# A hybrid decoder trunk in float32: one MLP weight block in four gets its remainder from an accumulating DMA instead of VectorE

## The chip, the cores and the metric

The kernel runs on one core of one Trainium2 chip. The metric is device microseconds of one execution. The profile is of one execution, recorded by the hardware; its times are microseconds from the first instruction unless ns is said. Engines: PE is TensorE (PEld its weight loads), DVE is VectorE, ACT is ScalarE, POOL is GpSimd, SP is SyncE, which here issues only DMAs.

## What is computed

Two decoder layers on 256 tokens of 2048 channels. Each layer mixes tokens with three parallel branches (convolution, recurrence, attention), adds their gated sum through one output projection, and then applies the part that this change touches:

```
h2 = rms_norm(x, mlp_norm_g[l])
x = x + jnp.square(jax.nn.relu(h2 @ w_mlp_up[l])) @ w_mlp_down[l]
```

`w_mlp_up` is 2048 x 8192 and `w_mlp_down` 8192 x 2048, in float32, for each layer.

## The kernel before

All matrix products are made in a rounded float32 type (`F32R`) that TensorE takes in one pass. To keep float32's precision each operand is split into a rounded part and its remainder: activations into `xhl`, `ah`, `yhl`, `oh` (both parts side by side, 512 columns), weights into `wh` (rounded part) and `wl` (remainder). For each tile of 128 weight rows there is a *pair* of products (`unit2`, through `mm`, line 154): `wh` times both activation parts, 512 columns, then `wl` times the rounded activation part, 256 columns.

Weights come in *blocks* of 128 x 1024 floats (512 KB), each good for eight pairs; there are 1034 loads in a run, 512 of them in the two MLPs. A block's way is `wload`: SP's queue loads it into a `raw` tile (L192), ScalarE copies it rounded into `wh` (through `act`, L150), VectorE subtracts, `wl = raw - wh` (through `tt`, L131). `raw`, `wh` and `wl` have four buffers each (`wpool`, `bufs=4`), and the program asks for blocks three ahead of their products (`AHEAD`). So a block may be rounded as soon as TensorE has made the last `wh` product with the block that held the buffer, four blocks earlier.

The MLP runs in quarters of its width (`MLP`: up 0, up 1, down 0, up 2, ...). A quarter has 16 output tiles, each made of two blocks, in PSUM tiles `pu` (four of them). After a tile of an up quarter, ScalarE and VectorE empty `pu` with three or four short operations (`s1`, `z`, `ah`); after a tile of a down quarter VectorE adds it to `x` with two. In the last down quarter ScalarE also squares `x` (`sq`) and GpSimd sums the squares (`ssq`, L316); the norm's factor follows from the sum (`rsqrt_cols`).

The order on each engine is not that of the text. A scheduler inside the framework (`schedule_with_timeline_sim=True`) sets it, engine by engine, before the program runs, and it also decides which free buffer a tile gets. On the chip each engine then takes its instructions strictly in that order.

Of the kernel before, what the change touches and what calls it, by code (L numbers as in the profile page):

```python
# [20 lines left out]
KT = D // 128  # L21
# [13 lines left out]
# columns of the packed per-layer vectors  # L35
P_CW, P_CB, P_LG, P_LB, P_RW, P_RB, P_BA, P_BX, P_LAM, P_PE, NPAR = 0, 124, 128, 132, 136, 160, 166, 172, 178, 184, 216
# columns of the packed constants
C_ID, C_COS, C_SIN, C_CAUS, C_MADD, C_M01, C_SEL, C_CMP, NCON = 0, 128, 384, 640, 768, 798, 828, 846, 906

# projection units (blocks of 128 columns of w_in) in the order of use  # L40
# [22 lines left out]
# where the loads of the compression go: after which gates, from which tile on, how many per tile  # L63
# [3 lines left out]
def _plan():  # L67
    """the order of the products: a branch's output projection starts DEFER tiles after its gates"""
    p = UNITS[:N_BRANCH]
    for n in "abc":  # L70
        k = 0
        for m in range(KT):
            p.append(("g" + n, m))
            if n == CMP_AT[0] and 0 <= m - CMP_AT[1] < 8 // CMP_AT[2]:
                for i in range(CMP_AT[2]):
                    i += (m - CMP_AT[1]) * CMP_AT[2]
                    p.append((("kc1", "vc1")[i // 4], i % 4))
            while m >= DEFER and k * (KT - DEFER) < (m + 1 - DEFER) * KT:
                p.append(("p" + n, k))
                k += 1  # L80
    return p
# [4 lines left out]
# weight loads in flight before their products; weight of side work in the pacing; its most per step on TensorE, us  # L86
AHEAD, SLACK, PE_SIDE = 3, 1.4, 0.4


@with_exitstack  # L90
def trunk(ctx: ExitStack, tc: tile.TileContext, a, out):
# [36 lines left out]
    # engine helpers, with a rough account of each engine's time for pacing the side work  # L128
# [30 lines left out]
    # ---- constants, per-layer vectors and the residual stream, [channel, token]  # L159
# [21 lines left out]
    # ---- weights: float32 blocks split exactly into a rounded part and its remainder, in a stream  # L181
    # that runs ahead of the products
    stream, ready = [], []

    def wload(src, n, parts=1):
        raw = wpool.tile([128, 1024], F32, tag="raw", name="raw")
        wh = wpool.tile([128, 1024], F32R, tag="wh", name="wh")
        wl = wpool.tile([128, 1024], F32R, tag="wl", name="wl")
        ready.append((wh, wl))
        for i in range(parts):  # L190
            c = slice(i * n // parts, (i + 1) * n // parts)
            nc.sync.dma_start(raw[:, c], src[:, c])  # L192
            act(wh[:, c], raw[:, c], AF.Copy)
            tt(wl[:, c], raw[:, c], f32(wh[:, c]), ALU.subtract)
# [6 lines left out]
    def split(dst, src, scale=None):  # L201
        """dst[:, 0] + dst[:, 1] = src (times scale), exactly up to float32's last bits"""
        if scale is None:
            act(dst[:, 0, :], src, AF.Copy)
            tt(dst[:, 1, :], src, f32(dst[:, 0, :]), ALU.subtract)
        else:
            act(dst[:, 0, :], src, AF.Copy, scale=scale)
            stt(dst[:, 1, :], src, scale, f32(dst[:, 0, :]), ALU.mult, ALU.subtract)

    def unit2(p, rhs):  # L210
        """p[:, :256] + p[:, 256:] = W^T rhs"""
# [15 lines left out]
    for l in range(L):  # L227
# [10 lines left out]
        for k, q in MLP:  # L238
            for m in range(KT):
                stream += halves(a["wup"][l, q * KT + m] if k == "up" else a["wdn"][l, q, m])  # L240

    # ---- side work that fills the engines beside the large products
# [32 lines left out]
    def prepare():  # L275
        """softplus(-lambda) and the scaled vectors, both layers at once"""
# [30 lines left out]
    def squares(m, pin=False):  # L307
        """adds the squares of x tile m"""
# [9 lines left out]
    def scaled(m, gcol):  # L318
        """the product of x tile m with the norm's gain as split parts"""
# [4 lines left out]
    def rsqrt_cols(tiles, n, raw=False):  # L324
        """(sum over channels of the tiles / n + eps) ** -0.5, per token: [token, 2] and on all partitions"""
# [17 lines left out]
    def causal_conv(o, u, w, b, k):  # L343
        """depthwise: o[t] = sum_j w[j] u[t - (k - 1 - j)] + b"""
# [36 lines left out]
    def rnn_task(l, rx, gg, rb_out):  # L381
        rw = par[:, l, P_RW:P_RW + 24]
        for m in range(6):
# [11 lines left out]
            # 1 - a = tanh(v/2) (1 + exp(-v)) with a = exp(-v)  # L395
# [20 lines left out]
    def gelu2(o, z, t):  # L416
        """o = 2 gelu(z), tanh form; t is scratch"""
# [13 lines left out]
    def compress(l, i, c, src, cz):  # L431
        """one load of the compression's first product: tokens 16 m + j of both heads, and the two position
        vectors, each as split parts, times the weights of positions j and 16 + j"""
# [21 lines left out]
    def attn_task(l, xs, rc, qn, kv, cz, oh):  # L455
        # branch gates, [token, head, branch]
# [29 lines left out]
        # values as [token, head dim], keys rotated  # L486
# [20 lines left out]
        # compressed keys and values  # L507
# [21 lines left out]
        # the compressed branch, all heads of a tile of queries at once  # L529
# [33 lines left out]
        # With these shapes the top-n selection takes every block and the window reaches over the whole  # L563
        # sequence, whatever the scores: both branches attend to all positions up to the query's.
# [52 lines left out]
    for l in range(L):  # L617
        # ---- token mixing: projections
# [85 lines left out]
        # ---- output projection  # L704
# [10 lines left out]
        # ---- squared-ReLU MLP, in quarters of its width  # L715
# [38 lines left out]
    # ---- final norm  # L754
# [8 lines left out]
def _blocks(w):  # L763
    """[2048, 128 n] -> [n, 2, 128, 1024]: for each block of 128 columns two loads, 8 tiles of rows each"""
# [4 lines left out]
def _rows(w):  # L769
    """[128 k, 128 n] -> [n, 128, 128 k]"""  # L770
# [4 lines left out]
def _cols(v):  # L775
    """per-channel vector(s) [..., c] -> [128, c / 128 ...]"""
# [81 lines left out]
```

## Time and profile before

| | |
|---|---|
| time, median of 3 runs | 2887.29 us (2886.95 to 2887.36) |
| span of the profiled execution | 2883.8 us |
| what lies around the span (median less span) | 3.5 us |
| PE, DVE, ACT, POOL busy, share of the span | 99%, 72%, 50%, 4% |
| DMA engines busy with the weight queue | 55.5% |

The span is from the first to the last recorded instruction of the one profiled execution; sums are made against it. An engine's busy share is an average over the whole program. A wait in the profile is the idle time of an engine just before an instruction, put down to what ended it. PE's matmuls are pipelined, so its recorded durations overlap; the distance between two starts is what a product costs.

### The profile page before, as it was taken

Reading aid. Unit: us, or ns where it says so; the run is one execution under the profiler, and the core shown is the slowest. Engines: PE = TensorE matmul, PEld = TensorE weight load, DVE = VectorE, ACT = ScalarE, POOL = GpSimd, SP = SyncE. Lnnn points to the kernel's source line nnn. Section 1 sums busy time; section 2 is a strip of 40 time slices with the busy share of each in tenths; the row PEclk is TensorE's granted clock in tenths of the full one; section 3 lists DMA queues with packets and bytes.
Section 4 is the critical chain, followed back from the end, with each engine's and each line's share of the span. In section 5 each row is a group of like instructions: output and inputs, shape, how many; then the busy total and the mean of one; then the engine's idle time right before and its main releaser. Section 6 shows DMA issues by size and latency. Waiting matters only on the chain.

```text
span 2883.8 us, 43174 instructions
## 1 busy us (share of the span) xinstructions
PE 2858.7 (99%) x16536; PEld 2504.1 (87%) x16536; DVE 2064.6 (72%) x3288; ACT 1455.8 (50%) x2206; POOL 109.6 (4%) x102
## 2 busy tenths in 40 slices
PE   8999999999999999999999999999999999999998
PEld 7888888888888888888888888888888888888887
DVE  7988866677676576666779787667776766756655
ACT  5448755555444344444544586455554444434443
POOL 2000000002000000000200000000020000000001
PEclk9999999999999999999999999999999999999999
DMA  6555654555555555555555556445555555555554
GB/s 222 190 185 172 206 166 149 177 196 190 184 190 191 190 190 190 190 190 190 190 189 190 180 181 214 142 153 183 195 191 185 190 190 190 190 190 190 190 190 139
DMA packets 152734, 534.15 MB, mean 185 GB/s; under 512 B 17232, under 2 KB 17488, under 8 KB 152528
## 3 DMA queue, kind: packets, MB, share of 16 engines
q1 hardware_dynamic: 151184, 528.23, 55.5%
q8 instruction: 129, 2.11, 0.3%
q0 software_dynamic: 768, 2.13, 0.2%
q10 hardware_dynamic: 576, 1.05, 0.1%
q14 instruction: 77, 0.63, 0.1%
HBM read 529.24 MB, written 2.10 MB: 184 GB/s over the span
## 4 chain that ended last, share of the span: by engine, by line
PE 98%; DMA 0%; DVE 0%; ACT 0%; POOL 0%; issue 0%; SPq 0%; POOLq 0%; DVEq 0%; ACTq 0%
PE pu L154 94%; PE pv L154 4%; POOL ssq L316 0%; PE pv L592 0%; DMA raw<-in_win_dram 0%; DVE fin L135 0%; DMA x<-in_xT_dram 0%; ACT wh L150 0%; ACT sq L150 0%; PE pv L558 0%; DVE wl L131 0%; PE pv L492 0%; DVE sw L131 0%; SPq L614 0%; DVE x L131 0%
## 5 line engine op out<-in xcount | busy, mean ns | idle before, releaser
L150 ACT ACTIVATE wh<-raw 128x1024 fp32r<-128x1024 f32 (+2 forms) x1034 | 1067.2, 1033 | 1321.0 <-PE pu L154 682.3
L131 DVE TENSOR_TENSOR wl<-raw,wh 128x1024 fp32r<-128x1024 f32 (+2 forms) x1034 | 1231.1, 1191 | 650.8 <-ACT wh L150 628.3
L154 PE MATMUL pu<-xhl,wh 128*128 128x512 f32 x4800 | 1680.9, 393 | 8.5 <-DVE xhl L135 8.5
L154 PE MATMUL pu<-xhl,wl 128*128 128x256 f32 x4800 | 1348.5, 281 | 1.2 <-DVE wl L131 1.1
L154 PEld LDWEIGHTS pu<-xhl,wh 128*128 128x128 f32 x4800 | 900.1, 188 | 207.7 <-DVE xhl L135 8.5
L154 PEld LDWEIGHTS pu<-xhl,wl 128*128 128x128 f32 x4800 | 908.5, 189 | 5.7 <-DVE wl L131 2.4
L154 PE MATMUL pu<-ah,wh 128*128 128x512 f32 x2048 | 710.2, 391 | 0.0
L154 PE MATMUL pu<-ah,wl 128*128 128x256 f32 x2048 | 573.4, 280 | 0.0
L154 PEld LDWEIGHTS pu<-ah,wh 128*128 128x128 f32 x2048 | 383.0, 187 | 84.0
L154 PEld LDWEIGHTS pu<-ah,wl 128*128 128x128 f32 x2048 | 387.1, 189 | 0.0
L131 DVE TENSOR_TENSOR x<-x,pu 128x256 f32<-128x256 f32 x320 | 134.4, 421 | 95.3 <-PE pu L154 90.0
L316 POOL TENSOR_TENSOR ssq<-ssq,sq 128x256 f32<-128x256 f32 x70 | 93.0, 1328 | 2255.0 <-ACT sq L150 2254.0
L154 PE MATMUL pu<-yhl,wh 128*128 128x512 f32 x512 | 177.5, 393 | 0.0
L154 PE MATMUL pu<-yhl,wl 128*128 128x256 f32 x512 | 141.7, 277 | 0.0
L154 PEld LDWEIGHTS pu<-yhl,wh 128*128 128x128 f32 x512 | 95.8, 187 | 22.0
L131 DVE TENSOR_TENSOR z<-pu,z 128x256 f32<-128x256 f32 x268 | 111.4, 417 | 0.6 <-ACT z L150 0.6
L135 DVE SCALAR_TENSOR_TENSOR cacc<-u,hpar,cacc 128x255 f32<-128x255 f32 (+14 forms) x240 | 103.7, 462 | 0.0
L150 ACT ACTIVATE z<-pu 128x256 f32<-128x256 f32 x268 | 97.9, 368 | 0.0
L154 PEld LDWEIGHTS pu<-yhl,wl 128*128 128x128 f32 x512 | 96.1, 188 | 0.2
L154 PE MATMUL pu<-oh,wh 128*128 128x512 f32 x192 | 67.4, 391 | 0.0
L131 DVE TENSOR_TENSOR z<-z,rb 128x256 f32<-128x256 f32 x136 | 57.7, 424 | 5.1 <-ACT rb L150 0.8
L135 DVE SCALAR_TENSOR_TENSOR s<-z 128x256 f32<-128x256 f32 x128 | 54.4, 425 | 4.5
(257 smaller groups left out, 1618.6 us busy)
## 6 DMA issues: line engine op xcount, KB each, us to landing
raw<-in_win_dram SPq DMA_DIRECT2D x342, 512.0 KB, 3.3
raw<-in_wup_dram SPq DMA_DIRECT2D x256, 512.0 KB, 4.2
raw<-in_wdn_dram SPq DMA_DIRECT2D x256, 512.0 KB, 4.3
raw<-in_wo_dram SPq DMA_DIRECT2D x64, 512.0 KB, 3.5
raw<-in_wro_dram SPq DMA_DIRECT2D x32, 384.0 KB, 3.1
raw<-in_wao_dram SPq DMA_DIRECT2D x32, 384.0 KB, 3.2
raw<-in_wco_dram SPq DMA_DIRECT2D x32, 256.0 KB, 3.2
raw<-in_cw_dram SPq DMA_DIRECT2D x16, 512.0 KB, 4.2
```

What stands on the lines that cost most here:

```text
L131: return V.tensor_tensor(o, x, y, op=op)
L135: return V.scalar_tensor_tensor(o, x, s, y, op0=op0, op1=op1)
L150: return A.activation(o, x, f, scale=scale, **kw)
L154: return T.matmul(o, l, r, start=start, stop=stop)
L316: G.tensor_tensor(ssq[0], ssq[0], q, op=ALU.add)
```

## The change

In `wload` a block may now get its remainder in another way. ScalarE copies `raw` twice: rounded into `wh`, and rounded with the opposite sign into `wl`. Then a DMA issued by GpSimd (POOL's queue) reads `raw` and adds it onto `wl` in place, element by element, so that `wl` holds `raw - wh` as before. VectorE has no part in such a block. The list of MLP blocks marks the second block of every even output tile: one in four, 8 in a quarter, 64 in a layer, 128 in all. Everything else is as it was (comments and blank lines aside, which shift line numbers: `act` is L152, `tt` L133, `mm` L156, the load L194, the adding DMA L199, GpSimd's sum L324).

```diff
+ADD_EVERY = 2
...
-    def wload(src, n, parts=1):
+    def wload(src, n, parts=1, adds=False):
...
             act(wh[:, c], raw[:, c], AF.Copy)
-            tt(wl[:, c], raw[:, c], f32(wh[:, c]), ALU.subtract)
+            if adds:
+
+                act(wl[:, c], raw[:, c], AF.Copy, scale=-1.0)
+                G.dma_start(out=f32(wl[:, c]), in_=raw[:, c], accum_op=ALU.add)
+            else:
+                tt(wl[:, c], raw[:, c], f32(wh[:, c]), ALU.subtract)
...
         for k, q in MLP:
             for m in range(KT):
-                stream += halves(a["wup"][l, q * KT + m] if k == "up" else a["wdn"][l, q, m])
+                first, second = halves(a["wup"][l, q * KT + m] if k == "up" else a["wdn"][l, q, m])
+                stream += [first, second + (1, m % ADD_EVERY == 0)]
```

The scheduler's order moves with it. TensorE, first up quarter of the first layer, the start of the second block of output tile 4 (`wh_7769` before, `wh_7771` after, an adding block after the change; `xhl_6772`, `xhl_6825` are the first activation tiles). Before:

```order
L154 MATMUL pu_7799<-xhl_7196,wh_7769 128x512
L154 MATMUL pu_7799<-xhl_7196,wl_7770 128x256
L154 MATMUL pu_7799<-xhl_7249,wh_7769 128x512
L154 MATMUL pu_7799<-xhl_7249,wl_7770 128x256
L154 MATMUL pu_7799<-xhl_7302,wh_7769 128x512
```

After:

```order
L156 MATMUL pu_7802<-xhl_7196,wh_7771 128x512
L156 MATMUL pu_7856<-xhl_6772,wh_7804 128x512
L156 MATMUL pu_7856<-xhl_6772,wl_7805 128x256
L156 MATMUL pu_7856<-xhl_6825,wh_7804 128x512
L156 MATMUL pu_7856<-xhl_6825,wl_7805 128x256
L156 MATMUL pu_7802<-xhl_7196,wl_7772 128x256
L156 MATMUL pu_7802<-xhl_7249,wh_7771 128x512
```

Between the first product with the rounded part and the first with the added remainder (`wl_7772`), two pairs of the next output tile (`pu_7856`) are pulled forward; at later adding blocks it is four, six, eight pairs, then two again, and none at the first two of a layer.

ScalarE at the same place. Before:

```order
L150 ACTIVATE wh_7769<-raw_7768 128x1024
L150 ACTIVATE s1_7736<-pu_7691 128x256
L150 ACTIVATE wh_7801<-raw_7800 128x1024
L150 ACTIVATE ah_7742<-s1_7736 128x256
L150 ACTIVATE wh_7823<-raw_7822 128x1024
```

After:

```order
L152 ACTIVATE wh_7771<-raw_7770 128x1024
L152 ACTIVATE s1_7738<-pu_7693 128x256
L152 ACTIVATE wl_7772<-raw_7770 128x1024
L152 ACTIVATE wh_7804<-raw_7803 128x1024
L152 ACTIVATE ah_7744<-s1_7738 128x256
```

The negated copy stands behind the rounded one, in the up quarters with one emptying of a PSUM tile between them; in the down quarters it follows directly.

SP's queue of loads in the same quarter, with the semaphores that each waits for (the adding DMAs' are named DMASW). Before:

```order
L192 DMA raw_7660<-in_wup_dram 128x1024 [waits DMAHW2_49,DVE_49]
L192 DMA raw_7692<-in_wup_dram 128x1024 [waits DMAHW3_49,DVE_49]
L192 DMA raw_7714<-in_wup_dram 128x1024 [waits DMAHW4_49,DVE_49]
L192 DMA raw_7746<-in_wup_dram 128x1024 [waits DMAHW5_49,DVE_49]
L192 DMA raw_7768<-in_wup_dram 128x1024 [waits DMAHW6_49,DVE_49]
```

After:

```order
L194 DMA raw_7661<-in_wup_dram 128x1024 [waits DMAHW3_49,DVE_49]
L194 DMA raw_7694<-in_wup_dram 128x1024 [waits DMAHW2_49,DMASW0_49]
L194 DMA raw_7716<-in_wup_dram 128x1024 [waits DMAHW4_49,DVE_49]
L194 DMA raw_7748<-in_wup_dram 128x1024 [waits DMAHW5_49,DVE_49]
L194 DMA raw_7770<-in_wup_dram 128x1024 [waits DMAHW7_49,DVE_49]
```

One load in four now waits for an adding DMA to finish reading its `raw` buffer, where it waited for VectorE's subtraction, and the loads behind it on SP's queue wait with it. It is the load five blocks after the adding one, not four: the scheduler gives the buffer that comes free late to the block after.

## Rows read from the trace of the kernel before

**Rows 1.** The page's busy time by engine, whole span.

```profile
span 2883.8 us, 43174 instructions
PE 2858.7 (99%) x16536; PEld 2504.1 (87%) x16536; DVE 2064.6 (72%) x3288; ACT 1455.8 (50%) x2206; POOL 109.6 (4%) x102
```

**Rows 2.** The waits view of PE, whole span: us in total, times, longest.

```profile
PE pu L154 <- DVE xhl L135: 8.5, 1, 8.5
PE pv L154 <- POOL ssq L316: 3.3, 1, 3.3
PE pv L154 <- ACT sq L150: 1.4, 1, 1.4
PE pu L154 <- DVE wl L131: 1.1, 2, 0.6
PE pv L154 <- POOL rc L333: 1.0, 1, 1.0
```

**Rows 3.** The windows view; 715 to 1424 and 2138 to 2853 are the MLPs.

```profile
core 0: us, PE busy (x) PEld busy (x) DVE busy (x) ACT busy (x) POOL busy (x), PEclk, DMA share, GB/s
0.00:715.00 715.00, 702.11 (x4055) 610.51 (x4056) 554.24 (x994) 410.57 (x702) 40.84 (x44) 1.00 0.56 185
715.00:1424.00 709.00, 709.00 (x4095) 625.05 (x4095) 476.17 (x657) 319.79 (x416) 19.55 (x15) 1.00 0.57 190
2138.00:2853.00 715.00, 715.00 (x4131) 630.34 (x4130) 470.35 (x648) 317.25 (x406) 20.98 (x16) 1.00 0.58 190
```

**Rows 4.** Timeline in a down quarter: start us, duration us, engine, operation, [idle before].

```profile
930.03 0.28 PE L154 MATMUL pu<-ah,wl 128*128 128x256 f32 x1
930.03 0.19 PEld L154 LDWEIGHTS pu<-ah,wh 128*128 128x128 f32 x1
930.15 0.39 PE L154 MATMUL pu<-ah,wh 128*128 128x512 f32 x1
930.15 0.19 PEld L154 LDWEIGHTS pu<-ah,wl 128*128 128x128 f32 x1
930.38 0.28 PE L154 MATMUL pu<-ah,wl 128*128 128x256 f32 x1
930.50 0.39 PE L154 MATMUL pu<-ah,wh 128*128 128x512 f32 x1
930.58 1.06 ACT L150 ACTIVATE wh<-raw 128x1024 fp32r<-128x1024 f32 x1 [1.71 <-PE pu L154]
...
933.35 1.06 ACT L150 ACTIVATE wh<-raw 128x1024 fp32r<-128x1024 f32 x1 [1.71 <-PE pu L154]
```

**Rows 5.** Timeline of ACT in an up quarter.

```profile
911.21 1.06 ACT L150 ACTIVATE wh<-raw 128x1024 fp32r<-128x1024 f32 x1 [1.41 <-issue]
912.18 0.36 ACT L150 ACTIVATE s<-pu 128x256 f32<-128x256 f32 x1
913.99 1.06 ACT L150 ACTIVATE wh<-raw 128x1024 fp32r<-128x1024 f32 x1 [1.44 <-issue]
```

**Rows 6.** Groups by form: busy us, mean ns of one, idle before.

```profile
L131 DVE TENSOR_TENSOR wl<-raw,wh 128x1024 fp32r<-128x1024 f32 x934 | 1145.3, 1226 | 603.8 <-ACT wh L150 582.8
L150 ACT ACTIVATE wh<-raw 128x1024 fp32r<-128x1024 f32 x934 | 990.8, 1061 | 1248.5 <-PE pu L154 662.5 <-issue 517.7 <-ACT xhl L150 44.3
L131 DVE TENSOR_TENSOR z<-pu,s 128x256 f32<-128x256 f32 x128 | 53.4, 417 | 0.0
L316 POOL TENSOR_TENSOR ssq<-ssq,sq 128x256 f32<-128x256 f32 x70 | 93.0, 1328 | 2255.0 <-ACT sq L150 2254.0
```

**Rows 7.** The loads' line (L192) between 900 and 1400: issue time, and issue to landing.

```profile
L192 SPq DMA_DIRECT2D raw<-in_wdn_dram x117: 327/328/328, 899.7 to 1398.9; - x117
...
DMA to landing us min/median/max: 3.1/4.3/4.5
```

**Rows 8.** GpSimd's own DMAs (L386, 128 KB each), whole span, the same columns.

```profile
L386 POOL DMA_DIRECT2D ruw<-in_rgw_dram x12: 536/547/719, 213.0 to 1698.6; - x12
...
DMA to landing us min/median/max: 2.3/3.3/4.4
```

**Rows 9.** The page's DMA queues (packets, MB, share of 16 engines) and an issue row.

```profile
q1 hardware_dynamic: 151184, 528.23, 55.5%
...
ruw<-in_rgw_dram POOLq DMA_DIRECT2D x12, 128.0 KB, 3.3
```

## The prediction, made before the changed kernel was timed

> **What bounds the kernel now.** I read the busy shares first, then PE's waits, then the windows, and last the timeline inside one window. TensorE is busy 99% of the span [rows 1], VectorE 72%. That VectorE is second says nothing yet; what counts is who waits for whom. PE's waits come to 15.3 us in the whole run, and the only ones for a remainder are two that make 1.1 us together [rows 2]. The windows settle it for the stage that is changed: in both MLPs PE is busy 709.00 of 709.00 and 715.00 of 715.00 us [rows 3]. The timeline shows the same from the other side: a pair of products takes 0.35 us (930.15 to 930.50), ScalarE rounds a block every 2.77 us, and each time it has sat idle for 1.71 us until TensorE released the buffer [rows 4]. TensorE sets the pace, at the full granted clock [rows 3], and everything else waits for it. A block is eight pairs, so a pair costs 2.77 / 8 = 0.346 us.
>
> **What the change removes.** 128 subtractions of 1.226 us on VectorE [rows 6], 157 us. None of it lies on the path: TensorE waits for no remainder in the MLPs [rows 2, 3]. The gain from this is 0.
>
> **What it adds on ScalarE.** 128 negated copies, priced as the rounded one, 1.061 us [rows 6]: 136 us, 68 in each MLP, where ScalarE is busy 320 of 709 us [rows 3]. It has room. The 1.4 to 1.7 us that it idles before a rounding [rows 4, 5] takes up the 1.06 us at the blocks concerned. On the path: 0.
>
> **What it adds on GpSimd.** 128 DMA issues. GpSimd's own issues take 0.55 us [rows 8], 70 us in all on an engine that is 4% busy [rows 1]. Behind one of them, at each MLP's start, stands the last addition of squares, which TensorE needs. From the release that starts ScalarE's work there: 2.5 us until the issue (below), 0.55, and 1.33 for the addition [rows 6], 4.4 us. In the new order TensorE asks for that sum some 8.4 us after the release (24 pairs). Covered, with 4 us left.
>
> **What it adds on the DMA engines.** A load is one pass over 512 KB: 55.5% of 2883.8 us for 528.23 MB [rows 9] is 1600 us for 1007 blocks' worth, 1.59 us a pass. An add reads `raw` and has to read what it adds to, so I bound it by one pass and by two: 128 x 1.59 to 3.18 = 204 to 407 us. In an MLP the engines are 57% busy [rows 3]; 64 adds make that 71% to 86%. Not full.
>
> **The term that decides: how long an add may take, and takes.** Call X the time from an add's issue to its landing.
>
> Allowed. The release is the last `wh` product that reads the buffer four blocks earlier. ScalarE starts 0.43 us after that product starts (930.15 and 930.58, [rows 4]). ScalarE's instructions follow each other at 0.97 us after a rounding [rows 5], so a negated copy ends 0.43 + 0.97 + 1.06 = 2.46 us after it in a down quarter, and at most 0.36 us later in an up quarter, where one emptying of PSUM stands between. Before, the first product with a new remainder came 25 pairs and one 512-column product after the start of the releasing one: 25 x 0.346 + 0.23 = 8.9 us. In the new order, counted at all 128 adds, it is 26 pairs in down quarters and 27 in up quarters as a rule (25.3 to 27.3): the pulled-forward pairs of the next tile delay the use, and part of that is taken back because the previous delay put off the release. That is 9.2 and 9.6 us. The weights must be loaded 0.12 us earlier. What is left for X is 9.2 - 0.1 - 2.5 = **6.6 us**, and the same in the up quarters.
>
> Taken. The trace has no adding DMA and none from SBUF to SBUF. The nearest rows are GpSimd's own 128 KB loads: 2.3 to 4.4 us to landing, median 3.3 [rows 8], and SP's 512 KB loads, 3.1 to 4.5 [rows 7]. Lower bound: the fastest of the former plus the three quarters of a pass that it lacks, 2.3 + 1.2 = 3.5 us. Upper bound: the slowest, the rest of the pass, a second pass, and one load that takes turns with it on every engine: 4.4 + 1.2 + 1.6 + 1.6 = 8.8 us. I take the median with a second pass, 3.3 + 1.2 + 1.6 = **6.1 us**: those rows already ran beside the loads, and no load is released by VectorE at an adding block, so the add meets fewer of them. 6.1 is under 6.6, but only just. Below zero the cost cannot go, since TensorE has no wait here to lose.
>
> The Trainium skill, in "Collectives: The Full Stack", section "The bandwidth ceiling: the fold count and why AG ≠ RS ≠ AR", says that the DMA engines' add itself is free but needs two source reads on the same ring, and so halves the rate (it gives 32.35 against 62.28 GB/s). No run here shows it yet. By it X is the 6.1 us above; by a single pass, as the trace's copies go, X would be 4.5 us and the margin 2 us.
>
> **What becomes late next.** The load that waits for an add goes out 2.5 + X after the release, lands 4.3 us later [rows 7], and needs 1.06 + 1.23 us [rows 6] for its split. Its first product comes at the earliest 17.3 us (50 pairs) after the same release. X may be 8.1 us before that is late: this binds after the first limit. The loads behind it on SP's queue move with it, and have more. The block whose pairs are pulled forward has 17 pairs, 6.1 us, where it had 25; it needs 0.43 + 0.97 + 1.23 = 2.6 us, or 3.9 with three short VectorE operations of 0.42 us ahead of it [rows 6]. Covered by 2 us. Changing tiles between pairs costs nothing that I can see: a weight load starts with the product before it, and even behind a 256-column product, 0.12 us, the next one starts on time [rows 4].
>
> **The sum.** 0 (VectorE) + 0 (ScalarE) + 0 (GpSimd) + 0 (adds under 6.6 us) = 0: span 2883.8, with the 3.5 us around it 2887.3 us, the median of before.
>
> **The rivals.**
>
> *Slower: the adds land late.* From X = 6.6 us on, TensorE stands at the first product with an added remainder, X - 6.6 us at each of 128, and nothing makes it up, since the next release moves too. At 7.7, midway to the upper bound, it is 1.1 x 128 = 141 us, 3028 us; at 8.8 it is 282 us, 3169 us. For it: the margin is half a microsecond on a price that no row shows. Against: the median row and both prices for the pass stay below it.
>
> *Slower: the DMA engines fill up.* Should an add cost three passes or more, four loads and an add need 7 x 1.59 = 11.1 us, which is what TensorE needs for four blocks (11.1 us). From there the engines are the bound; with four passes it is 12.7 us, 1.6 x 128 = 205 us, 3092 us. Against: two reads and a write side by side are the two passes above.
>
> *Faster: TensorE's own pace rises with less traffic from VectorE.* 0.2% needs 0.4% in the MLPs. Against: 702.11 us for 4055 products before the MLP, with VectorE busy 554 of 715 us, and 709.00 for 4095 in it, with 476 of 709 [rows 3], are both 0.173 us a product.
>
> That the change does not do what it says I leave out: the order shows 64 adding DMAs on GpSimd in each layer.
>
> **How the numbers follow.** A measurement of this kernel can tell about 0.2% (5.8 us) from no change. No change 0.60; adds late 0.31; DMA engines full 0.05; faster 0.04. So faster 0.04, same 0.60, slower 0.36. The likeliest is 2887.3 us, with its own range of 2882 to 2893. The range has to reach into the late adds: about half of them, up to X = 7.7, which is 3028. From 2882 to 3030 us leaves out some 0.15 to 0.18 above and next to nothing below.
>
> **What the profile will show.** Right, if PE is busy through both MLPs without a wait for `wl`, the adds' time to landing lies under 6.6 us, VectorE's busy time falls by about 157 us and ScalarE's rises by about 136, and the DMA share in the MLPs is 70 to 86%. Wrong, if PE waits for a DMA into `wl` 128 times; then that wait, divided by 128, is X less what was allowed. If PE waits for `wh` instead, the load behind the add was late.

## The result: slower by 21.6 us, and one product of an adding block waits for its add

| | before | after |
|---|---|---|
| time, median of 3 runs | 2887.29 us | 2908.88 us (2905.76 to 2910.83) |
| ratio, 95% interval | | 1.0074 [1.0054, 1.0093] |
| span of the profiled execution | 2883.8 us | 2904.0 us |

By the 0.2% that the prediction set as the bound, this is slower. The forecast was no change. The page of the changed kernel, its first lines and its queues:

```profile
span 2904.0 us, 43514 instructions
PE 2878.3 (99%) x16536; PEld 2505.0 (86%) x16536; DVE 1906.0 (66%) x3160; ACT 1566.8 (54%) x2334; POOL 213.6 (7%) x230
...
q1 hardware_dynamic: 151184, 528.23, 52.8%
q0 software_dynamic: 19200, 69.25, 13.3%
```

Against [rows 1]: VectorE lost 158.6 us, TensorE is still busy 99% of the span, with the same 16536 products, and its busy time grew by 19.6 us of the span's 20.2. So TensorE waited hardly more; the same products took longer. PE's waits say it again, beside [rows 2] (us in total, times, longest):

```profile
PE pu L156 <- DVE xhl L137: 8.8, 1, 8.8
PE pv L156 <- POOL ssq L324: 3.3, 1, 3.3
PE pv L156 <- ACT sq L152: 1.4, 1, 1.4
PE pv L156 <- POOL rc L341: 1.0, 1, 1.0
PE pu L156 <- DVE wl L133: 0.8, 2, 0.4
PE pu L156 <- DMA wl<-raw: 0.7, 1, 0.7
```

The last line is the only wait of a product for an add among 128 of them: 0.7 us, up to 2546.51 us. The adding DMAs themselves, by their line (issue time, then issue to landing), beside [rows 7, 8]:

```profile
L199 POOL DMA_DIRECT2D wl<-raw x128: 839/852/919, 729.5 to 2875.3; - x128
...
DMA to landing us min/median/max: 4.5/4.8/6.6
```

The windows view of the two MLPs, over the same stretches as [rows 3] (us, then busy time and instruction count of PE, PEld, DVE, ACT, POOL, granted clock, DMA share, GB/s):

```profile
715.00:1424.00 709.00, 709.00 (x4046) 617.39 (x4046) 392.39 (x586) 368.94 (x471) 67.81 (x75) 1.00 0.78 232
2138.00:2853.00 715.00, 714.26 (x4075) 621.71 (x4074) 389.90 (x581) 365.98 (x464) 66.67 (x74) 1.00 0.77 232
```

PE is as full as before, at the same granted clock of 1.00, and yet 4046 products fit where [rows 3] had 4095, and 4075 where there were 4131. Those 49 and 56 products, at 0.173 us each, are 8.5 and 9.7 us: 18.2 of the 20.2 us by which the span grew, the wait of 0.7 among them. The loss is in TensorE's own pace, spread over the MLPs.

To compare kernels I use one measure from here on: the products in 600 us of the first MLP, 800 to 1400. Before:

```profile
800.00:1400.00 600.00, 600.00 (x3463) 529.03 (x3462) 397.85 (x548) 265.54 (x337) 8.37 (x6) 1.00 0.57 190
```

After:

```profile
800.00:1400.00 600.00, 600.00 (x3418) 522.07 (x3417) 327.14 (x490) 306.70 (x384) 49.39 (x57) 1.00 0.78 234
```

A pair is two products: 1200 / 3463 = 346.5 ns before, 1200 / 3418 = 351.1 ns after. In the starts of the single products, 351.1 turns out to be a mixture of two paces. In one a pair takes 346.7 ns: 230 ns behind the 512-column product, 117 behind the 256-column one, or nearly so. In the other it takes 353.3 ns: three pairs run 241, 120, 236, 113, 233, 117 ns, and begin again. Stretches of either, some 10 us long or less, follow each other, and the pace changes at the pulled-forward pairs. Here is one such place in the timeline of PE (start us, duration us; the line with x2 is two 512-column products in a row, the first of tile m's second block and the first of tile m + 1):

```profile
1005.82 0.40 PE L156 MATMUL pu<-xhl,wh 128*128 128x512 f32 x1
1006.05 0.28 PE L156 MATMUL pu<-xhl,wl 128*128 128x256 f32 x1
1006.17 0.62 PE L156 MATMUL pu<-xhl,wh 128*128 128x512 f32 x2
1006.63 0.28 PE L156 MATMUL pu<-xhl,wl 128*128 128x256 f32 x1
1006.74 0.40 PE L156 MATMUL pu<-xhl,wh 128*128 128x512 f32 x1
1006.98 0.28 PE L156 MATMUL pu<-xhl,wl 128*128 128x256 f32 x1
```

Up to it the pairs run at the fast pace; from 1006.98 on, for more than 10 us, at the slow one. The kernel before runs at the fast pace from 744.4 us to the end of its first MLP without a break.

Theory: the scheduler's new order costs the time, not the adds. Rival: the adds cost it, by their traffic or by waits too short to count.

### The profile page after: what moved, and what is told of

Its sections match the earlier page's. It is cut to its first block, busy times and chain, and to the rows that moved or that the text cites. A ratio compares the mean times of both kernels' runs of the same rounds, so it can differ in the third digit from the quotient of the medians.

```text
span 2904.0 us, 43514 instructions
## 1 busy us (share of the span) xinstructions
PE 2878.3 (99%) x16536; PEld 2505.0 (86%) x16536; DVE 1906.0 (66%) x3160; ACT 1566.8 (54%) x2334; POOL 213.6 (7%) x230
## 3 DMA queue, kind: packets, MB, share of 16 engines
q0 software_dynamic: 19200, 69.25, 13.3%
## 4 chain that ended last, share of the span: by engine, by line
PE 97%; DMA 1%; issue 1%; DVE 0%; ACT 0%; POOL 0%; SPq 0%; POOLq 0%; DVEq 0%; ACTq 0%
PE pu L156 93%; PE pv L156 4%; POOL ssq L324 0%; PE pv L600 0%; DMA raw<-in_win_dram 0%; DMA x<-in_xT_dram 0%; DMA wl<-raw 0%; ACT wh L152 0%; DVE fin L137 0%; DMA raw<-in_wdn_dram 0%; ACT sq L152 0%; DVE wl L133 0%; PE pv L566 0%; PE pv L500 0%; DVE sw L133 0%
## 5 line engine op out<-in xcount | busy, mean ns | idle before, releaser
L152 ACT ACTIVATE wh<-raw 128x1024 fp32r<-128x1024 f32 (+2 forms) x1034 | 1065.3, 1031 | 1220.1 <-PE pu L156 757.8
L156 PE MATMUL pu<-xhl,wh 128*128 128x512 f32 x4800 | 1685.8, 396 | 8.8 <-DVE xhl L137 8.8
L133 DVE TENSOR_TENSOR wl<-raw,wh 128x1024 fp32r<-128x1024 f32 (+2 forms) x906 | 1075.6, 1187 | 586.0 <-ACT wh L152 572.6
L156 PE MATMUL pu<-xhl,wl 128*128 128x256 f32 x4800 | 1339.2, 281 | 0.9 <-DVE wl L133 0.8
L156 PEld LDWEIGHTS pu<-xhl,wh 128*128 128x128 f32 x4800 | 897.6, 188 | 211.3 <-DVE xhl L137 8.8
L156 PEld LDWEIGHTS pu<-xhl,wl 128*128 128x128 f32 x4800 | 908.2, 189 | 10.7 <-DVE wl L133 2.1
L156 PE MATMUL pu<-ah,wh 128*128 128x512 f32 x2048 | 715.0, 397 | 0.0
L156 PE MATMUL pu<-ah,wl 128*128 128x256 f32 x2048 | 563.3, 280 | 0.7 <-DMA wl<-raw 0.7
L156 PEld LDWEIGHTS pu<-ah,wh 128*128 128x128 f32 x2048 | 380.2, 188 | 87.6
L156 PEld LDWEIGHTS pu<-ah,wl 128*128 128x128 f32 x2048 | 386.3, 189 | 7.1 <-DMA wl<-raw 1.3
L133 DVE TENSOR_TENSOR x<-x,pu 128x256 f32<-128x256 f32 x320 | 134.0, 419 | 185.2 <-PE pu L156 179.9
L199 POOL DMA_DIRECT2D wl<-raw x128 | 108.9, 851 | 1243.7 <-ACT wl L152 1179.8
L156 PE MATMUL pu<-yhl,wh 128*128 128x512 f32 x512 | 177.5, 393 | 0.0
L324 POOL TENSOR_TENSOR ssq<-ssq,sq 128x256 f32<-128x256 f32 x70 | 89.5, 1279 | 930.6 <-ACT sq L152 924.8
L133 DVE TENSOR_TENSOR z<-pu,s 128x256 f32<-128x256 f32 x128 | 53.8, 421 | 143.3 <-ACT s L152 143.3
L156 PE MATMUL pu<-yhl,wl 128*128 128x256 f32 x512 | 141.7, 277 | 0.0
L152 ACT ACTIVATE wl<-raw 128x1024 fp32r<-128x1024 f32 x128 | 133.6, 1044 | 0.0
L156 PEld LDWEIGHTS pu<-yhl,wh 128*128 128x128 f32 x512 | 95.8, 187 | 22.0
L133 DVE TENSOR_TENSOR z<-pu,z 128x256 f32<-128x256 f32 x268 | 111.4, 418 | 0.6 <-ACT z L152 0.6
L152 ACT ACTIVATE z<-pu 128x256 f32<-128x256 f32 x268 | 97.7, 367 | 0.0
L156 PEld LDWEIGHTS pu<-yhl,wl 128*128 128x128 f32 x512 | 96.2, 188 | 0.2
```

What stands on the lines that cost most here:

```text
L133: return V.tensor_tensor(o, x, y, op=op)
L152: return A.activation(o, x, f, scale=scale, **kw)
L156: return T.matmul(o, l, r, start=start, stop=stop)
L199: G.dma_start(out=f32(wl[:, c]), in_=raw[:, c], accum_op=ALU.add)
L324: G.tensor_tensor(ssq[0], ssq[0], q, op=ALU.add)
```

## Experiments

All ratios are against the kernel before on the same chip. What differs between the kernels is the order of the products in the MLPs and the adds, together or apart.

### The order of after without an add, and the adds without its order

`order_as_after` is the kernel before, with the MLP products issued in the order that the changed kernel has. `keep` holds the instructions given to it in program order on their engine. From before (`prod` is one product, `run` whole pairs, `p0` and `p1` two output tiles; `PAIRS` is the list of the changed kernel's pulls, 64 per layer):

```diff
+    PAIRS = (0, 0, 2, 4, 6, 8, 2, 4, 6, 8, 2, 4, 6, 8, 2, 4, 6, 7, 8, 2, 3, 4, 5, 6, 7, 8.5, 3, 5, 7, 8.5, 3, 5, 7, 8, 2, 3, 4, 5, 6, 7, 8, 2, 4, 6, 8, 2, 4, 6, 8, 2, 3, 4, 5, 6, 7, 8, 2, 3, 4, 5, 6, 7, 8, 2)
...
+        run(p0, wnext(), 0, 8, 0)
+        w = wnext()
+        prod(p0, w, 0, 8, False)
+        p1 = big_ps()
+        v = wnext()
+        n = int(pairs)
+        run(p1, v, 0, n, 0)
...
+        prod(p0, w, 0, 8, True)
+        run(p0, w, 1, 8, 8)
```

`adds_in_order` is the changed kernel with its MLP products held in program order, which gives the order of before. From after:

```diff
-                mm(p, h, r.rearrange("p a s -> p (a s)"), k == 0, False)
-                mm(p[:, :S], lo, r[:, 0, :], False, k == n - 1)
+                i1 = mm(p, h, r.rearrange("p a s -> p (a s)"), k == 0, False)
+                if pin:
+                    keep(i1)
+                i2 = mm(p[:, :S], lo, r[:, 0, :], False, k == n - 1)
+                if pin:
+                    keep(i2)
```

Expected of the first:

> The kernel before, all remainders by VectorE and no adding DMA, with TensorE's products of the MLP pinned to exactly the order that the scheduler gave the changed kernel (0, 2, 4, 6, 8 ... pairs of the next tile pulled forward). Order theory: 351 ns a pair in the MLP windows and 2905 to 2910 us. Traffic theory: 347 ns a pair and 2887 to 2889 us.

Measured: 2905.26 us, ratio 1.0065 [1.0048, 1.0082], with 3417 products in the 600 us, as after has 3418:

```profile
800.00:1400.00 600.00, 600.00 (x3417) 522.05 (x3416) 386.66 (x544) 261.08 (x333) 6.99 (x5) 1.00 0.58 187
```

The order alone, with no add in the kernel, brings 18.3 of the 21.6 us.

Expected of the second:

> The changed kernel, adds and all, but TensorE's products of the MLP are pinned to the order of the text, which is the order of the kernel before. Order theory (pulling pairs of the next tile forward slows TensorE's own pace, 353 instead of 347 ns a pair): no pulled-forward pairs, so 347 ns a pair throughout and 2887 to 2890 us. Adds land 4.5 to 6.6 us after issue and 6.3 us are allowed in this order, so at most a wait or two. Traffic theory (the adding DMAs' reads and writes of SBUF slow TensorE's reads): about 2908 us again, 350 ns a pair in the MLP windows.

Measured: 2900.07 us, ratio 1.0047 [1.003, 1.0063], and its four runs scatter from 2894.19 to 2906.25. Neither theory as I had put it: the order of before is back, and most of the loss is still there. Its trace (a run of 2906.25 us) shows where. The timeline of the first MLP, the weight loads (PEld) of one place among the products:

```profile
758.27 0.39 PE L156 MATMUL pu<-xhl,wh 128*128 128x512 f32 x1
...
758.50 0.28 PE L156 MATMUL pu<-xhl,wl 128*128 128x256 f32 x1
...
758.61 0.39 PE L156 MATMUL pu<-xhl,wh 128*128 128x512 f32 x1
...
758.94 0.19 PEld L156 LDWEIGHTS pu<-xhl,wl 128*128 128x128 f32 x1 [0.25 <-DMA wl<-raw]
758.94 0.39 PE L156 MATMUL pu<-xhl,wl 128*128 128x256 f32 x1
```

One weight load waits 0.25 us for an add, which was issued at 753.00 us and took 5.9 to land. The next stands at 2542.61 us in the second MLP (a third, 0.19 us at 735.32, falls among the first tiles, ahead of the windows below); here the add landed in 5.1 us, but GpSimd issued it 1.6 us after ScalarE's copy had ended, where the median is 0.3, for no reason that the profile shows (timeline of ACT, POOL and PEld):

```profile
2534.79 1.04 ACT L152 ACTIVATE wl<-raw 128x1024 fp32r<-128x1024 f32 x1
...
2537.42 0.84 POOL L199 DMA_DIRECT2D wl<-raw  x1 [11.26 <-issue]
...
2542.61 0.19 PEld L156 LDWEIGHTS pu<-ah,wl 128*128 128x128 f32 x1 [0.52 <-DMA wl<-raw]
```

That late issue is no accident of one run: the same add, the 98th, goes out 1.6 us after its copy in the traces of after (2540.27 us), `adds_three` (2529.30) and `adds_lead` (2524.64) too, and it is the add that the one waiting product of after waits for.

And the windows behind the first wait, ahead of the second, and behind it:

```profile
760.00:1400.00 640.00, 640.00 (x3625) 554.95 (x3624) 351.69 (x522) 332.05 (x414) 52.73 (x61) 1.00 0.79 233
2200.00:2540.00 340.00, 340.00 (x1964) 299.78 (x1963) 196.00 (x305) 184.44 (x242) 26.29 (x31) 1.00 0.80 236
2545.00:2880.00 335.00, 335.00 (x1898) 290.56 (x1898) 169.90 (x240) 168.00 (x194) 38.50 (x42) 1.00 0.80 231
```

640 us for 3625 products is 353.1 ns a pair, 340 for 1964 is 346.2, 335 for 1898 is 353.0. The adds go on alike in all three windows, with DMA shares of 0.79 and 0.80; the pace differs by what happened at the two waits. A quarter of a microsecond was followed by 640 us at the slow pace. So a second theory: either pace, once entered, stays until the next disturbance, and a disturbance can be a pulled pair or a short wait. Where a wait falls differs between executions, which would explain the scatter of the four runs.

### How many pairs are pulled

`order_2` and `order_3`: no adds, and from the fifth tile of an MLP on, in every second tile always two, or always three pairs of the next tile pulled forward. The code is that of `order_as_after` with one number for all places, 2 here and 3 in `order_3`:

```diff
+    AHEAD_PAIRS = 2
...
+        run(p1, v, 0, AHEAD_PAIRS, 0)
```

> The kernel before with always two pairs of the next tile pulled forward in the second block of every even tile (not in the first four tiles of a layer's MLP), no adds. In the changed kernel's trace most stretches behind a two-pair pull run at 353 ns. Order theory: 353 ns a pair in nearly all of both MLPs, 3840 pairs times 6.6 ns = 25 us, 2912 us. Traffic theory: 2887 us.

> As with two pairs, but always three. In the changed kernel's trace the stretches behind a three-pair pull run at 346.6 ns. Order theory, if the number of pulled pairs decides the pace that follows: 347 ns nearly everywhere and 2887 to 2891 us. If any pull slows TensorE: 2905 to 2912 us. Traffic theory: 2887 us.

Measured: 2910.8 us, ratio 1.0083 [1.0068, 1.0098], with 3405 products in the 600 us; and 2889.79 us, ratio 1.0011 [1.0001, 1.002], with 3456. The windows of `order_2`, then of `order_3`:

```profile
800.00:1400.00 600.00, 600.00 (x3405) 521.29 (x3404) 386.30 (x541) 261.55 (x330) 5.62 (x4) 1.00 0.57 186
800.00:1400.00 600.00, 600.00 (x3456) 524.06 (x3454) 392.45 (x549) 267.40 (x337) 8.38 (x6) 1.00 0.59 190
```

Two kernels with the same pulls at the same places, one pair apart in length, differ by 21 us. The cost is not in the pull; it is in the pace that it leaves behind. With three pairs, the pace is slow inside the pull and fast again behind it, 346.9 ns a pair up to the next pull; with two it stays slow behind it, 353.1 ns.

### One pull, two pulls, and the way back

If the pace stays, then a few pulls should do for a whole MLP. No adds in these four, and the order of before but for the named places. `one_pull`, from `order_2`, with the number of pairs as an argument:

```diff
-                two_tiles(xs, lambda j, p: empty(m + j, p))
+                two_tiles(xs, lambda j, p: empty(m + j, p), 2 if qi == 0 and m == 4 else 0)
...
-                two_tiles(hq[qi], lambda j, p: empty(m + j, p))
+                two_tiles(hq[qi], lambda j, p: empty(m + j, p), 0)
```

`two_pulls` has `m in (4, 6)` for `m == 4`. `pull_and_back` and `pulls_and_back` are `one_pull` and `two_pulls` with one more pull, in the first tile of down quarter 0, of three pairs in layer 0 and six in layer 1:

```diff
-                two_tiles(hq[qi], lambda j, p: empty(m + j, p), 0)
+                two_tiles(hq[qi], lambda j, p: empty(m + j, p), (3, 6)[l] if qi == 0 and m == 0 else 0)
```

> The kernel before, without any accumulating DMA, whose products run in its own order but for one place in each layer's MLP: in tile 4 of up quarter 0 two pairs of tile 5 are pulled in front of a product with the remainder, as the changed kernel does at 128 places. In the run with the adds in program order the pace of the pairs went from 0.347 to 0.353 us at one wait of 0.25 us (at 758.9 us) and did not come back in the 660 us that were left of that MLP. Theory 'the slow pace, once entered, stays until something resets it': 124 of the 128 tiles of each MLP go slow, about 124 x 16 pairs x 6.65 ns = 13.2 us a layer, 26.4 us in all, time about 2913 us, TensorE's count of products in 715 to 1424 us falls to some 4,030. Rival 'each pull costs its own few tenths of a microsecond': two pulls, time 2887 to 2888, and the pace is back within a tile or two.

> As the run with one pull of two pairs in each MLP, and 28 tiles later, in the first tile of down quarter 0, a second pull: of three pairs in layer 0, of six in layer 1. In the changed kernel the stretches behind pulls of three and six pairs ran at the fast pace. Theory 'a pull of three or six pairs resets the pace, whatever it was before': slow for 28 tiles of each layer alone, 2 x 28 x 16 x 6.65 ns = 6.0 us, time about 2893. Rival 'the pace behind a pull hangs on the pace ahead of it' (three pairs keep a slow pace as they keep a fast one): no return, time 2913, or one layer returns and the other does not: about 2903. If one pull does nothing that lasts: 2888.

Measured: 2886.66 us, ratio 0.9998 [0.9989, 1.0008], and 2886.9, ratio 0.9999 [0.999, 1.0009]; 3464 products in the 600 us in both. A miss: one pull of two pairs costs nothing and leaves the pace fast, and pulls of three or six behind it keep it so. But the single intervals changed: ahead of the pull each pair was 230 and 117 ns, behind it the pairs took turns at about 232 and 118, 231 and 112, 233 and 117, 231 and 113, still 346.7 on average. There are two fast patterns, and in `order_2`, too, the first pull led from the first into the second; its slow pace began at the second pull. So I did the two alone:

> The kernel before, without adds, with two pulls of two pairs in each layer's MLP (in tile 4 and in tile 6 of up quarter 0), and its own order elsewhere. With one pull (tile 4) the pace stayed at 0.347 us a pair, only the intervals within it changed (from 230/117 ns to 232/118 and 231/113 ns); in the order with a pull of two pairs in every second tile, too, the slow pace began at its second pull and not at its first. Theory 'a pull of two pairs takes the first fast pattern into the second and the second into the slow one, and each stays until the next disturbance': slow from tile 7 on, 121 tiles x 16 pairs x 6.65 ns = 12.9 us a layer, time 2886.9 + 25.8 = about 2913, some 4,030 products in 715 to 1424 us. Rival 'the slow pace needs pull after pull': 2887 to 2888 and the fast pace behind the second pull or a tile later.

> As the run with two pulls of two pairs in each MLP, and a third pull 26 tiles after the second, in the first tile of down quarter 0: three pairs in layer 0, six in layer 1. Theory 'the pattern behind a pull hangs on the pattern ahead of it': in the changed kernel's trace a pull of six pairs led from the slow pace back to the fast one, so layer 1 is slow for some 26 tiles (26 x 16 x 6.65 ns = 2.8 us) and fast from there; three pairs are half a turn of it and were seen from a fast pattern alone, so layer 0 may stay slow (12.9 us): time about 2903; 2893 if both pulls lead back, 2913 if neither does. If two pulls do nothing that lasts: 2888.

Measured: 2913.36 us, ratio 1.009 [1.0075, 1.0105], and 2892.7 us, ratio 1.002 [1.0011, 1.0029]. Windows of `two_pulls`, from behind the second pull on:

```profile
774.00:1400.00 626.00, 626.00 (x3546) 542.98 (x3545) 407.80 (x565) 272.44 (x348) 5.60 (x4) 1.00 0.57 186
```

Windows of `pulls_and_back`, between the second pull and the third, and behind the third, in layer 0 (three pairs), then in layer 1 (six pairs):

```profile
774.00:917.00 143.00, 143.00 (x812) 124.09 (x811) 99.57 (x151) 68.83 (x102) 0.00 (x0) 1.00 0.57 186
921.00:1400.00 479.00, 479.00 (x2766) 418.91 (x2765) 311.44 (x417) 207.09 (x251) 7.36 (x6) 1.00 0.59 190
2203.00:2346.00 143.00, 143.00 (x811) 124.10 (x811) 99.73 (x151) 68.83 (x102) 0.00 (x0) 1.00 0.56 186
2351.00:2850.00 499.00, 499.00 (x2881) 436.45 (x2880) 318.79 (x426) 213.60 (x255) 12.42 (x9) 1.00 0.58 190
```

With two pulls: 1252 / 3546 = 353.1 ns a pair, for the 626 us of the window, with not one further change of order. 26.2 us are lost to a few products that changed places at two points of each MLP, where 25.8 were expected. With the third pull the pace goes from 286 / 812 = 352.2 ns to 958 / 2766 = 346.3 in layer 0 and to 998 / 2881 = 346.4 in layer 1. I had thought that three pairs might not lead back; both did. The theory holds: the pace behind a disturbance hangs on the pattern ahead of it and on the disturbance, and then it stays. The trace of after says so too, against what I expected of six pairs: behind a pull of six the pace is 352.8 ns from 828.74 us on, and 347.0 from 997.38 on, though ahead of both pulls it was slow (353.3 and 353.5).

### The adds without a wait

`adds_lead` is `adds_in_order` with one change: in a block with an add, ScalarE makes the negated copy first, and each add starts about one copy earlier.

```diff
-            act(wh[:, c], raw[:, c], AF.Copy)
             if adds:
-                act(wl[:, c], raw[:, c], AF.Copy, scale=-1.0)
+                keep(act(wl[:, c], raw[:, c], AF.Copy, scale=-1.0))
                 G.dma_start(out=f32(wl[:, c]), in_=raw[:, c], accum_op=ALU.add)
+                keep(act(wh[:, c], raw[:, c], AF.Copy))
             else:
+                act(wh[:, c], raw[:, c], AF.Copy)
```

> The changed kernel with its products pinned to the order of the kernel before (as in the run with the adds in program order), and in a block with an add ScalarE makes the negated rounded part first and the rounded part behind it, so that each add starts one ScalarE copy (1.04 us) earlier. In the run without this, two waits for an add, of 0.25 and 0.5 us, stood at the two places where the pace of an MLP went slow. Theory 'the adds themselves cost nothing, it is the order or a wait that sets the slow pace': with no product waiting for an add both MLPs stay fast, time 2886 to 2890, and some 4,090 products or more in 715 to 1424 us. Rival 'the adds' traffic (DMA engines 0.79 busy) slows the products or brings on the slow pace by itself': about 2900 to 2908 as before, with slow stretches that begin where no product waits.

Measured: 2886.36 us over ten runs, ratio 1.0003 [0.9994, 1.0012]. All 128 adds are in it:

```profile
800.00:1400.00 600.00, 600.00 (x3464) 529.03 (x3463) 336.27 (x492) 315.85 (x390) 52.27 (x60) 1.00 0.79 237
```

```profile
DMA to landing us min/median/max: 4.5/5.1/6.1
```

The first fence is the window, the second the landing of the adds. 3464 products, with VectorE relieved of the same work and the DMA engines as full (0.79) as after the change. No product waits for an add in either MLP. One of the ten runs took 2896.74 us; it has no trace, and a wait late in one MLP would fit. So the traffic of 128 adds costs nothing that can be measured, and what is left of the changed kernel's loss is the order, with now and then a wait.

### A wait on purpose

`wait_once` is `adds_lead` with one late block in each MLP: a second DMA adds a tile of 128 x 128 zeros (`zero`) behind the add of tile 6.

```diff
+                if adds > 1:
+                    G.dma_start(out=f32(wl[:, :128]), in_=zero, accum_op=ALU.add)
...
-                stream += [first, second + (1, m % ADD_EVERY == 0)]
+                stream += [first, second + (1, (m % ADD_EVERY == 0) + ((k, q, m) == ("up", 0, 6)))]
```

> The adds with their earlier start and the products in the order of the kernel before (2886.4 us, no product waits for an add), and at one block of each MLP, the second of tile 6 of up quarter 0, a second accumulating DMA behind the first, which adds a small tile of zeros (128 x 128) to the columns of the block's first product: that product has to wait once, by my estimate some 0.5 to 3 us. Theory 'one wait is enough to set the slow pace, and it stays': the two waits and 2 x 121 x 16 x 6.65 ns = 25.8 us, about 2914 (half of it, 2901, if the pace goes slow in one layer and not in the other, since the pattern behind a wait may hang on its length). Rival 'a wait costs its own length and no more, and the slow stretches in the run with the adds in order come from the traffic': 2887 to 2892.

Measured: 2913.64 us, ratio 1.0093 [1.0077, 1.011], which is the 2914 expected, but the trace does not show the sum that I had made of it. Waits, then windows behind the wait of layer 0, behind that of layer 1, and the long stretches behind each:

```profile
PE pu L156 <- DMA wl<-zero: 7.9, 2, 4.0
```

```profile
777.00:779.00 2.00, 2.00 (x8) 1.71 (x7) 0.00 (x0) 0.00 (x0) 0.00 (x0) 0.50 0.19 76
779.00:781.00 2.00, 2.00 (x12) 1.72 (x11) 0.33 (x1) 0.74 (x2) 0.00 (x0) 0.81 0.00 0
```

```profile
2208.00:2210.00 2.00, 2.00 (x8) 1.71 (x8) 0.00 (x0) 0.00 (x0) 0.00 (x0) 0.50 0.57 229
2210.00:2212.00 2.00, 2.00 (x8) 1.71 (x7) 0.00 (x0) 0.00 (x0) 0.00 (x0) 0.50 0.00 0
2212.00:2214.00 2.00, 2.00 (x9) 1.72 (x9) 0.85 (x2) 1.33 (x3) 0.00 (x0) 0.66 0.00 0
```

```profile
785.00:1400.00 615.00, 615.00 (x3550) 537.88 (x3549) 346.00 (x510) 324.62 (x403) 52.37 (x60) 1.00 0.78 237
2220.00:2850.00 630.00, 630.00 (x3568) 546.56 (x3567) 342.44 (x505) 324.22 (x399) 53.93 (x62) 1.00 0.78 233
```

The waits were 4 us, longer than I had estimated. Around the end of each the granted clock fell to 0.50, the 1.2 GHz level, for some microseconds: 8 products in 2 us. After that layer 0 went on at 1230 / 3550 = 346.5 ns a pair, fast, and layer 1 at 1260 / 3568 = 353.1, slow to the end. So one wait can set the slow pace and it stays (layer 1), but not every wait does (layer 0), as the expectation's half case had it. The total came out as expected because the longer waits and the low clock made up for the layer that stayed fast: against `adds_lead` the profiled span grew by 26.7 us (2911.2 from 2884.5), of which the waits are 7.9 and the slow pace of layer 1 in the window 630 x (1 - 346.5 / 353.1) = 11.8. Product by product, the starts in the two traces divide it further: layer 0's wait with the low clock behind it costs 5.7 us, layer 1's 6.9, the slow pace from there to the last product 12.9; the other 1.2 lie outside the MLPs.

### The adds behind three pulled pairs

`adds_three` is `order_3` with `wload` and the marked blocks of the changed kernel:

```diff
+                first, second = halves(a["wup"][l, q * KT + m] if k == "up" else a["wdn"][l, q, m])
+                stream += [first, second + (1, m % ADD_EVERY == 0)]
```

> The changed kernel's adds (128 of them, as it has them) with the products in a fixed order: in every second tile three pairs of the next tile are pulled in front of the first product that needs the added remainder (the order that without adds took 2889.8 us). The add has 1 us more time than in the kernel before's order. Theory 'order and waits alone': no product waits for an add, the fast pace is kept, time 2889 to 2892. Rival 'the adds' traffic costs something of its own': the difference between the changed kernel (2908.9) and its order without adds (2905.3), 3.6 us, comes on top: 2893 to 2894. If a wait for an add turns up all the same, the pace behind it may go slow until the next pull: up to 2900.

Measured: 2891.93 us, ratio 1.0018 [1.0009, 1.0028], with 3455 products in the 600 us where `order_3` had 3456. It is inside what order and waits give (2889 to 2892), at its upper end; PE waited once for an add, 0.8 us up to 2535.09 us, and behind this wait the pairs ran at 230 and 117 ns, the fast pace. But the rival's 2893 lies inside the scatter of the ten runs (2891.13 to 2893.45), so this run alone does not decide between the two.

### Twice as many adds

`adds_half` is `adds_lead` with an add for the second block of every tile, half of the MLPs' blocks.

```diff
-ADD_EVERY = 2
+ADD_EVERY = 1
```

> The adds with their earlier start, products pinned to the order of the kernel before, and twice as many of them: the second block of every tile, half of the MLPs' blocks. With 128 adds the DMA engines are 0.78 busy in the MLPs against 0.58 without, so 256 adds ask for 0.98. Theory 'an add is 1.9 passes of its bytes': the share comes out at 0.95 to 1.00, loads and adds run late, products wait for them and the slow pace comes with the waits: 2900 to 2960, the landing of an add well over 5.1 us. Rival 'an add is one pass, the rest of the share is its waiting': a share under 0.9, no waits, 2886 to 2890.

Measured: 2987.11 us, ratio 1.0343 [1.0328, 1.0358], above the range given. The window, PE's wait for the adds, their landing, and their queue on the page:

```profile
800.00:1400.00 600.00, 581.19 (x3264) 498.93 (x3263) 257.12 (x417) 344.29 (x417) 86.55 (x102) 1.00 0.99 268
```

```profile
PE pu L156 <- DMA wl<-raw: 54.3, 57, 2.5
```

```profile
DMA to landing us min/median/max: 4.5/6.6/9.5
```

```profile
q0 software_dynamic: 37632, 136.37, 25.0%
```

Now the DMA engines are full, 0.99 busy, and the products wait 57 times: 54.3 of the 99.8 us by which the span grew over that of `adds_lead`. The rest I have not divided. An add takes 0.25 x 2984.3 / 256 = 2.9 us of all 16 engines, 1.8 passes of the 1.59 us that the prediction worked out from [rows 9].

## The prediction, point by point

- **What bounds the kernel.** Right: TensorE, before without a wait in the MLPs, after with the one of 0.7 us.
- **VectorE's 157 us, worth 0.** Right: 158.6 us went away and the time did not fall with them, in `adds_lead` either.
- **ScalarE's 136 us, hidden.** Right in effect. The 128 negated copies took 133.6 us, 1044 ns each, and ScalarE's busy time grew by 111.0, since a copy overlaps its neighbours.
- **GpSimd's issue at 0.55 us.** Mis-sized: 0.852 us, so its busy time grew by 104 us and not by 70. It changed nothing: the wait for the squares is 3.3 us as in [rows 2].
- **DMA engines at 71% to 86%.** Right: 0.78 and 0.77. The queue's 13.3% of 2904.0 us over 128 adds is 3.0 us each, 1.9 passes, close to the two of the upper bound. The Trainium skill's rule ("Collectives: The Full Stack", section "The bandwidth ceiling: the fold count and why AG ≠ RS ≠ AR"), that an add needs two source reads, agrees with these 1.9 passes.
- **X, the landing of an add: 6.1 us, between 3.5 and 8.8.** Mis-sized on the safe side: the median is 4.8 us. The term too many is the second pass of 1.6 us: it shows in the share of the DMA engines, but not in the landing, where the sum without it is 4.5. The allowance was mis-sized the other way: the copy of `adds_in_order` that ended at 752.70 us had its add issued at 753.00, and these 0.3 us were not in my sum, so 6.6 was 6.3. The maximum of after is 6.6, and one product waited 0.7 us, for the add that was issued 1.6 us late and took 6.2. In the order of before the product that waits at 758.94 was due at 758.69, 5.7 us after the issue, and the median of 4.7 us left room; what made products wait in `adds_in_order` was one slow landing and one late issue, which a median does not show.
- **The load behind the add binds later.** Right as far as can be seen: PE waits for no `wh` in either trace.
- **"Changing tiles between pairs costs nothing that I can see."** This is the step that failed. What I looked at in [rows 4] was whether a weight load starts on time behind a short product, and it does. I did not ask whether the pace of the products behind the change would be the same, and it is not: 351.1 ns a pair for 346.5. The new order got no term in the sum. Over 2048 pairs in each of two MLPs that is 4.6 ns x 4096 = 18.8 us, for a measured growth of the span of 20.2 and of the median of 21.6; `order_as_after` shows 18.3 of it with no add in the kernel. The trace of before could have warned me: ahead of its first MLP, from 385.6 to 394.9 us, its pairs run at the slow pace. These two starts are nine pairs apart, 3.18 / 9 = 0.353 us a pair, with no wait between them:

```profile
386.78 0.40 PE L154 MATMUL pu<-xhl,wh 128*128 128x512 f32 x1
...
389.96 0.40 PE L154 MATMUL pu<-xhl,wh 128*128 128x512 f32 x1
```

- **The rivals.** The late adds came once, for 0.7 us, and not 128 times. Full DMA engines did not come; they need about twice as many adds (`adds_half`). The faster pace did not come either. That rival looked at TensorE's own pace and in one direction only: both stretches of [rows 3] that I compared, 0.173 us a product each, run mostly at the same pace, so their agreement said nothing of whether there is another.
- **The range.** It reached 3030 us for late adds. 2908.9 lies in it for another reason; the likeliest case's own range, 2882 to 2893, does not hold it.

What stays open: why TensorE has these two paces, and a rule for which disturbance leads where. The traces show the transitions, not their cause. The remaining 3.6 us between the medians of the changed kernel and `order_as_after` are 1.2 in the two profiled spans (2904.0 and 2902.8), 0.7 of which is the one wait; the runs of after scatter by 5 us, and I can't divide it further.

No kernel here beats the one before: its MLPs run at the fast pace already, and `adds_lead`, which takes the same work off VectorE, is equal to it.

## What to carry to other kernels

When a change lets a scheduler move the instructions of the engine that bounds the kernel, the new order is an edit of its own: count that engine's instructions in a fixed window before and after, and price the order by itself, with the old data flow in the new order. Where the bounding engine has no wait to lose, look at what one instruction costs, since a loss can hide in a busy share that stays at 100%. Hold the slowest transfer against the slack, not the median, when a quarter of a microsecond of waiting can be followed by hundreds of microseconds at another pace.

## What I had not expected of the hardware

- TensorE ran alternating products of 512 and 256 columns at two steady paces, 346.5 and 353.1 ns a pair, 1.9% apart, at a granted clock of 1.00 in both. Each stays for as long as nothing disturbs it: the slow one for 640 us in `adds_in_order`, the fast one for 680 us in the kernel before.
- The pace can be changed by a single wait of 0.25 us (to slow, 758.9 us in `adds_in_order`), by a second pull of two pairs (to slow, `two_pulls`), and by pulls of three or six pairs (back to fast, `pulls_and_back`; behind six pairs in after it is fast at some places and slow at others). Not every wait changes it (`adds_three`, layer 0 of `wait_once`), and the first pull of two pairs changes only the pattern within the fast pace.
- Around the end of a wait of 4 us without a product, the granted clock fell to 0.50 for some microseconds (`wait_once`, 777 to 779 and 2208 to 2212 us); in the second case it was 1.00 again from 2214 on.
- An accumulating DMA of 512 KB from one SBUF tile onto another took 0.85 us to issue, 4.5 to 6.6 us from issue to landing beside a stream of loads, and about 3.0 us of all 16 DMA engines. GpSimd issued one of them, the 98th in each of four kernels, 1.6 us after ScalarE's copy had ended, where 0.3 us was the median.
